# Routing and gathering the first 128 tokens while the second 128 are still being mapped, in an encoder trunk with experts

## The chip, the cores and the metric

The kernel runs on one core of one Trainium2 chip. Its engines are named as the profile names them: PE (matrix products, with PEld for the loading of its weights), DVE (the vector engine), ACT (the scalar engine), POOL (the general engine) and SP, which only issues transfers. The metric is the device time of one execution in microseconds (us). Three executions of the kernel before took 1431.76, 1432.56 and 1432.91 us; the median, 1432.56 us, is the time that the change is compared with. The profiled execution, from which all rows below come, took 1431.94 us, and its span in the trace is 1430.1 us.

## The reference, cut to what matters

Two layers act on 256 tokens of 1024 features. Layer 0 (retention and a dense SwiGLU) isn't touched apart from one small insertion. Layer 1 mixes the tokens by a two-dimensional Fourier transform with a linear map behind it, adds that to the residual, normalises, and sends each token to 2 of 8 experts:

```python
h = h + fourier_mixer(hn, fnet_w_out[j])          # the map: y.reshape(b, s, d) @ w_out
hn = rms_norm(h, ffn_norm[i])                     # y * rsqrt(mean(x^2) + eps) * g
h = h + moe_swiglu(hn, moe_router[j], moe_w_gate[j], moe_w_up[j], moe_w_down[j])

def moe_swiglu(h, w_router, w_gate, w_up, w_down):
    t = h.reshape(-1, d)
    logits = (t @ w_router).astype(jnp.float32)
    top_val, top_idx = lax.top_k(logits, TOP_K)
    top_w = jax.nn.softmax(top_val, axis=-1)
    gates = jnp.sum(jax.nn.one_hot(top_idx, N_EXPERTS) * top_w[..., None], axis=1)
    for e in range(N_EXPERTS):
        out = out + gates[:, e:e + 1] * swiglu(t, w_gate[e], w_up[e], w_down[e])
```

The norm's factor rsqrt(...) is one number for each token, so it changes neither which experts are largest nor their order; the kernel picks the experts from the rows multiplied by the gain g alone and puts the factor into the gates and the expert products later.

## The kernel before, in words

All arithmetic is float32 in two parts: a value is split into a high part (ACT copies it to the rounded type, `whi`, `nhi`, `xe`...) and a low part (DVE subtracts: `wlo`, `nlo`...), and a product is three matmuls, high by high, high by low, low by high (`mm3`, L247 to L250). The weights stream in pieces of 1 MB ("items" here). SP issues the transfer of an item as soon as one of its 11 to 15 buffers is free, ACT and DVE split an item in two halves each (L131, L132) into one of three pairs of buffers, and PE then takes 12 matmuls of 512 columns for it. There is no scheduler: each engine works its instructions in the order in which the code writes them, and waits where an operand is not there.

The tokens stand in two chunks of 128, c = 0 and 1, and the features in two halves of 512, hf = 0 and 1. The part around the change comes in this order.

- The map (`close`, L319). The last two items of `fnet_w_out` are applied group by group: (c, hf) = (0,0), (0,1), (1,0), (1,1), 12 matmuls each. After a group DVE adds its result to the residual `X` and multiplies it by the gain (`gained`, L261 to L268). One group later `r_sink` (L809) turns the gained half by four PE transposes, ACT copies them out (`xt`), ACT and DVE split the gained half into `nh`, `nl`, and ACT sums its squares. Two groups later the router's products run (`r_mm`, L768: four f32 matmuls of 8 columns, two passes each).
- The routing (`route`, L775): eight small DVE operations for a chunk find its two largest experts and write `mask`. PE counts, by a matmul with the triangular `upper`, the place `pos` of each token in its expert's list (L825 to L830); chunk 1 continues chunk 0's count through `ones`. `gates` (L786) works out the weights of the experts by some 20 tiny POOL operations.
- The gathering of the first two experts' tokens (`prep(0)`, L919): `choose` (L840) writes the 0/1 matrices `pm` on DVE, four tiles of 128x128; `gather` (L849) multiplies them with `nh` and `nl`, quarter by quarter (q = 0 to 3, each with both chunks, 8 matmuls of 256 columns), and splits each quarter into `xe`. All these tiles are in a pool `pe` that takes the memory of the pool before it, `pc`, and waits for all users of that pool.
- The experts, 56 steps of 512 hidden features (L1089 on). A step takes two items for the gate, two for the up product and two for the step before it down. The last part of `prep(0)`, `place` (L860: eight small passes that carry the gates to the gathered tokens), is run in step 0, between the first and the second item (L1104).

Of the kernel before, what the change touches and what calls it, by code (L numbers as in the profile page):

```python
# [12 lines left out]
OP = mybir.AluOpType  # L13
# [139 lines left out]
def body(nc, tc, a, out, upto=None):  # L153
    with ExitStack() as ctx:
# [76 lines left out]
        def route_consts(rw):  # L231
            nc.scalar.dma_start(rw, a["moe_router"][0].rearrange("(k p) e -> p k e", p=P))
            kw = dict(base=0, allow_small_or_imprecise_dtypes=True)
            ge.iota(iota8, pattern=[[1, NE]], channel_multiplier=0, **kw)
            ge.iota(slot, pattern=[[1, P]], channel_multiplier=0, **kw)
            ge.memset(ones, 1.0)
# [24 lines left out]
        def gained(c, hf, accs=None):  # L261


            x = X[:, c, HALF[hf]]
            if accs is not None:
                ve.tensor_add(x, x, accs[2 * c + hf])
            ve.tensor_mul(xgs[hf], x, gb[:, HALF[hf]])
            return xgs[hf]  # L268
# [50 lines left out]
        def close(its, accs, sink, early=None):  # L319
# [15 lines left out]
            return lambda: sink(*left)  # L335

# [272 lines left out]
        with tc.tile_pool(name="pb", bufs=1) as pb:  # L609
# [3 lines left out]
            tabd = pb.tile([P, 2, 512], F32, name="tabd", tag="hth", bufs=2)  # L613
            accs = [acc(i) for i in range(4)]
# [25 lines left out]
            for u in range(6):  # L640
# [22 lines left out]
                if u == 1:  # L663
                    split(td[0], td[1], tabd)
                hms[u] = []
# [35 lines left out]
        with tc.tile_pool(name="pc", bufs=1) as pc:  # L701
# [64 lines left out]
            sq, late = sq_tile(), []  # L766
# [42 lines left out]
            def r_sink(c, hf, xg):  # L809
                p = tr()  # L810
                for k in range(4):
                    te.transpose(p[:, cp(k)], xg[:, cp(k)], ident)
                se.copy(xt[c][:, 4 * hf:4 * hf + 4], p.rearrange("p (k t) -> p k t", k=4))
                for ch in late:
                    r_mm(*ch)
                late[:] = [(c, hf)]
                split(nh[:, c, HALF[hf]], nl[:, c, HALF[hf]], xg)
                square(sq, c, hf)

            left = close(its, accs, r_sink)  # L820
            po = mm("po")
            route(0)
            left()
            r_mm(1, 1)
            te.matmul(po[:, 0:8], upper, mask[:, 0], start=True, stop=True)  # L825
            route(1)
            ve.tensor_copy(pos[:, 0], po[:, :8])
            te.matmul(po[:, 8:16], ones, mask[:, 0], start=True, stop=False)
            te.matmul(po[:, 8:16], upper, mask[:, 1], start=False, stop=True)
            ve.tensor_copy(pos[:, 1], po[:, 8:16])  # L830
            gates()

# [5 lines left out]
        with tc.tile_pool(name="pe", bufs=1) as pe, tc.tile_pool(name="dr", bufs=1, space=bass.MemoryType.DRAM) as dr:  # L838
            pe = Aligned(pe)
            def choose(e0):  # L840

                pm = pe.tile([P, 2, 2 * P], F32R, name="pm")
                for c in range(2):
                    for j in range(2):
                        ve.tensor_scalar(pm[:, c, cp(j)], slot, pos[:, c, e0 + j:e0 + j + 1],
                                         mask[:, c, e0 + j:e0 + j + 1], op0=OP.is_equal, op1=OP.mult)
                return pm

            def gather(pm, xe, q, o=None):  # L849

                o = o or mm("ga")
                for i in range(2):
                    ds = cp(2 * q + i)
                    for c in range(2):
                        te.matmul(o[:, i * 256:(i + 1) * 256], nh[:, c, ds], pm[:, c], start=c == 0, stop=False)  # L855
                        te.matmul(o[:, i * 256:(i + 1) * 256], nl[:, c, ds], pm[:, c], start=False, stop=c == 1)  # L856
                ov = o.rearrange("p (i j s) -> p j i s", i=2, j=2)
                split(xe[:, :, 0, 2 * q:2 * q + 2], xe[:, :, 1, 2 * q:2 * q + 2], ov)

# [59 lines left out]
            def prep(e0):  # L919

                st = {}

                def first():
                    st["pm"] = choose(e0)
# [279 lines left out]
```

## Time and profile before

| | before |
|---|---|
| median of three runs | 1432.56 us |
| the profiled execution | 1431.94 us, span 1430.1 us |
| busy share of the span: PE, PEld, DVE, ACT, POOL | 98%, 82%, 81%, 68%, 5% |
| bytes read from memory | 431.54 MB |

The page's share of busy time is an average over stages that have different limits. PE is busy in nearly all of the span, so the reader looks for two things: the few places in which it isn't, and the places in which it works at a lower granted clock. A timeline row gives the start in us from the span's start, the duration in us (of all of the row's instructions, x how many), the engine, the line, the operation, output<-inputs and shape, and in brackets how long the engine had been idle and what ended it. Matmuls are pipelined: a duration is longer than the distance to the next start, and it is this distance that a matmul costs.

### The profile page before, as it was taken

The numbers are of one execution on the slowest core, as the hardware profiler recorded it, in microseconds if no ns is written. First come the engines' busy times: TensorE is split into PE (matmuls) and PEld (weight loads), VectorE is DVE, ScalarE is ACT, GpSimd is POOL, SyncE is SP. The second block draws the span as 40 slices with busy tenths as digits, with TensorE's granted clock in tenths as the row PEclk, the third lists the DMA queues.
The fourth block names the chain that finished last, engine by engine and source line by source line (L and its number), as shares of the span: only waits on it lengthen the run. The fifth ranks groups of instructions, "written<-read, shape, count | busy, mean of one in ns | idle before, by whom it ended". The sixth has DMA issues, their size and how long they took to land. (4 is left out here: it accounts for less than half of the span.)

```text
span 1430.1 us, 17313 instructions
## 1 busy us (share of the span) xinstructions
PE 1405.9 (98%) x6533; PEld 1166.7 (82%) x6533; DVE 1164.9 (81%) x1201; ACT 969.8 (68%) x1120; POOL 70.2 (5%) x109
## 2 busy tenths in 40 slices
PE   7999999999999999999999999999999999999997
PEld 6888878888888888888888888887878888888786
DVE  6866666545577999989999988998988898999996
ACT  5544446444455777777877777787777778778775
POOL 8400000000001000000000000000000000001000
PEclk9999999999999999999999999999999999999999
DMA  8646539755536989999999999999999999999990
GB/s 288 213 154 205 177 132 375 251 179 200 181 120 243 385 302 358 371 356 340 334 394 393 386 361 364 362 347 390 348 373 361 356 373 366 393 383 346 395 347 30
DMA packets 186700, 437.45 MB, mean 306 GB/s; under 512 B 8161, under 2 KB 10993, under 8 KB 186610
## 3 DMA queue, kind: packets, MB, share of 16 engines
q1 hardware_dynamic: 181424, 426.27, 81.7%
q10 hardware_dynamic: 4610, 7.92, 1.5%
q0 software_dynamic: 576, 2.10, 0.4%
q8 instruction: 52, 0.85, 0.2%
q14 instruction: 38, 0.31, 0.1%
HBM read 431.54 MB, written 4.72 MB: 305 GB/s over the span
## 5 line engine op out<-in xcount | busy, mean ns | idle before, releaser
L132 DVE TENSOR_TENSOR wlo<-raw,whi 128x1024 fp32r<-128x1024 f32 (+1 forms) x789 | 923.5, 1219 | 148.3 <-ACT whi L131 139.9
L131 ACT CAST whi<-raw 128x1024 fp32r<-128x1024 f32 (+1 forms) x789 | 786.1, 1047 | 200.7 <-PE acc L250 106.3
L248 PE MATMUL mm<-whi,xe 128*128 128x512 f32 x896 | 355.1, 396 | 0.3 <-PEq L1129 0.3
L250 PE MATMUL mm<-whi,xe 128*128 128x512 f32 x896 | 349.6, 390 | 0.0
L249 PE MATMUL mm<-wlo,xe 128*128 128x512 f32 x896 | 349.2, 390 | 0.0
L249 PE MATMUL acc<-wlo,hth 128*128 128x512 f32 x528 | 206.3, 391 | 2.3 <-DVE wlo L132 2.3
L248 PE MATMUL acc<-whi,hth 128*128 128x512 f32 x528 | 206.2, 391 | 0.0
L250 PE MATMUL acc<-whi,htl 128*128 128x512 f32 x528 | 206.1, 390 | 0.0
L250 PEld LDWEIGHTS mm<-whi,xe 128*128 128x128 f32 x896 | 168.2, 188 | 36.1
L248 PEld LDWEIGHTS mm<-whi,xe 128*128 128x128 f32 x896 | 168.4, 188 | 34.9 <-issue 2.2
L249 PEld LDWEIGHTS mm<-wlo,xe 128*128 128x128 f32 x896 | 168.5, 188 | 32.9
L248 PE MATMUL mm<-whi,nhi 128*128 128x512 f32 (+1 forms) x352 | 135.6, 385 | 0.0
L250 PE MATMUL mm<-whi,nlo 128*128 128x512 f32 (+1 forms) x352 | 133.9, 380 | 0.0
L249 PE MATMUL mm<-wlo,nhi 128*128 128x512 f32 (+1 forms) x352 | 133.7, 380 | 0.0
L249 PEld LDWEIGHTS acc<-wlo,hth 128*128 128x128 f32 x528 | 99.5, 188 | 23.3 <-DVE wlo L132 2.8
L250 PEld LDWEIGHTS acc<-whi,htl 128*128 128x128 f32 x528 | 99.5, 188 | 20.7
L248 PEld LDWEIGHTS acc<-whi,hth 128*128 128x128 f32 x528 | 99.6, 189 | 20.6
L253 ACT CAST hth<-tr 128x512 fp32r<-128x512 f32 (+1 forms) x67 | 38.9, 581 | 84.8 <-PE tr L294 84.8
L250 PEld LDWEIGHTS mm<-whi,nlo 128*128 128x128 f32 x352 | 66.2, 188 | 12.9
L249 PEld LDWEIGHTS mm<-wlo,nhi 128*128 128x128 f32 x352 | 66.3, 188 | 11.8
L248 PEld LDWEIGHTS mm<-whi,nhi 128*128 128x128 f32 x352 | 66.3, 188 | 11.9
L254 DVE TENSOR_TENSOR htl<-tr,hth 128x512 fp32r<-128x512 f32 (+1 forms) x67 | 45.7, 682 | 33.5 <-ACT hth L253 33.5
(291 smaller groups left out, 992.6 us busy)
## 6 DMA issues: line engine op xcount, KB each, us to landing
raw<-in_moe_w_gate SPq DMA_DIRECT2D x110, 1024.0 KB, 7.6
raw<-in_moe_w_down SPq DMA_DIRECT2D x108, 1024.0 KB, 7.6
raw<-in_moe_w_up SPq DMA_DIRECT2D x105, 1024.0 KB, 7.3
raw<-in_ret_w_in SPq DMA_DIRECT2D x23, 1024.0 KB, 5.2
raw<-in_dense_w_gate SPq DMA_DIRECT2D x11, 1024.0 KB, 5.3
raw<-in_dense_w_up SPq DMA_DIRECT2D x11, 1024.0 KB, 8.8
raw<-in_dense_w_down SPq DMA_DIRECT2D x11, 1024.0 KB, 6.6
raw<-in_ret_w_out SPq DMA_DIRECT2D x8, 1024.0 KB, 4.9
```

The source lines that it names most:

```text
L131: self.nc.scalar.copy(hi[sl], t[sl])
L132: self.nc.vector.tensor_sub(lo[sl], t[sl], hi[sl].bitcast(F32))
L248: te.matmul(o, lh, rh, start=first, stop=False)
L249: te.matmul(o, lh, rl, start=False, stop=False)
L250: te.matmul(o, ll, rh, start=False, stop=last)
L253: se.copy(hi, src)
L254: ve.tensor_sub(lo, src, hi.bitcast(F32))
```

## The change

The close of the map, the routing and the first gathering are written out as one sequence in which chunk 0 is ahead. `r_t` transposes `X` itself and not the gained half; to make up for that, the gain vector is loaded as 8 rows (`rg`), turned by one small PE transpose and multiplied into the router's weights during the dense layer. The gain product of chunk 1 goes to POOL (`gained(..., ge)`). `choose` and `gather` work on one chunk at a time: chunk 0's `mask`, `pos`, `pm` and its half of all four gathers run before chunk 1 is routed; three matmuls without a use (`warm`) stand ahead of chunk 1's half of the gathers. The `pm` of these gathers lies in the older pool `pt`, and POOL writes a second `pm` in pool `pe` for `place`, which runs behind the second item of step 0 and not behind the first. Pool `pe` is opened with `reuse_waits="tile"`: each of its tiles waits only for the users of its own bytes.

```diff
--- before.py
+++ after.py
@@ -230,6 +230,7 @@
 
         def route_consts(rw):
             nc.scalar.dma_start(rw, a["moe_router"][0].rearrange("(k p) e -> p k e", p=P))
+            nc.scalar.dma_start(rg[:8], a["ffn_norm"][1].rearrange("(k p) -> k p", p=P))
             kw = dict(base=0, allow_small_or_imprecise_dtypes=True)
             ge.iota(iota8, pattern=[[1, NE]], channel_multiplier=0, **kw)
             ge.iota(slot, pattern=[[1, P]], channel_multiplier=0, **kw)
@@ -258,13 +259,12 @@
             se.activation(hi, src, AF.Copy, scale=s)
             ve.scalar_tensor_tensor(lo, src, s, hi.bitcast(F32), op0=OP.mult, op1=OP.subtract)
 
-        def gained(c, hf, accs=None):
+        def gained(c, hf, accs, eng=None):
 
 
             x = X[:, c, HALF[hf]]
-            if accs is not None:
-                ve.tensor_add(x, x, accs[2 * c + hf])
-            ve.tensor_mul(xgs[hf], x, gb[:, HALF[hf]])
+            ve.tensor_add(x, x, accs[2 * c + hf])
+            (eng or ve).tensor_mul(xgs[hf], x, gb[:, HALF[hf]])
             return xgs[hf]
 
         scr = []
@@ -333,6 +333,19 @@
                         sink(*left)
                     left = (c, hf, xg)
             return lambda: sink(*left)
+
+        def choose(pm, e0, c, eng=None):
+
+            for j in range(2):
+                (eng or ve).tensor_scalar(pm[:, c, cp(j)], slot, pos[:, c, e0 + j:e0 + j + 1],
+                                          mask[:, c, e0 + j:e0 + j + 1], op0=OP.is_equal, op1=OP.mult)
+
+        def gather(o, pm, q, c):
+
+            for i in range(2):
+                ds = cp(2 * q + i)
+                te.matmul(o[:, i * 256:(i + 1) * 256], nh[:, c, ds], pm[:, c], start=not c and not i, stop=False)
+                te.matmul(o[:, i * 256:(i + 1) * 256], nl[:, c, ds], pm[:, c], start=False, stop=bool(c and i))
 
         def run(hooks, i):
             for f in hooks.get(i, ()):
@@ -611,6 +624,7 @@
             scratch(pb)
             tabr = pb.tile([P, 2, 2 * H1], F32, name="tabr")
             tabd = pb.tile([P, 2, 512], F32, name="tabd", tag="hth", bufs=2)
+            rg = pb.tile([P, P], F32, name="rg")
             accs = [acc(i) for i in range(4)]
             rst, sq = [], sq_tile()
 
@@ -662,6 +676,9 @@
                 o = dense_h(u)
                 if u == 1:
                     split(td[0], td[1], tabd)
+                    p = tr()
+                    te.transpose(p[:, :8], rg[:8], ident[:8, :8])
+                    ve.tensor_mul(rw, rw, p[:, :8, None].to_broadcast([P, 8, NE]))
                 hms[u] = []
                 for c in range(2):
                     t = pb.tile([P, 512], F32, name="hm", bufs=3)
@@ -763,7 +780,7 @@
 
             xt = [pc.tile([P, 8, P], F32, name="xt", tag="fh", bufs=2) for _ in range(2)]
             lgp = [mm("lg") for _ in range(2)]
-            sq, late = sq_tile(), []
+            sq = sq_tile()
 
             def r_mm(c, hf):
                 for k in range(4 * hf, 4 * hf + 4):
@@ -806,57 +823,87 @@
                 ge.tensor_add(gts[:, :, :NE], gts[:, :, :NE], g2)
                 ge.tensor_copy(gts[:, :, NE], rs)
 
-            def r_sink(c, hf, xg):
+            def maps(c, hf, i):
+                it, lh, ll = its[i]
+                out_mm(accs, it, lh, ll, c, False, i == 1, (hf,))
+
+            def r_t(c, hf):
+
                 p = tr()
                 for k in range(4):
-                    te.transpose(p[:, cp(k)], xg[:, cp(k)], ident)
+                    te.transpose(p[:, cp(k)], X[:, c, cp(4 * hf + k)], ident)
                 se.copy(xt[c][:, 4 * hf:4 * hf + 4], p.rearrange("p (k t) -> p k t", k=4))
-                for ch in late:
-                    r_mm(*ch)
-                late[:] = [(c, hf)]
-                split(nh[:, c, HALF[hf]], nl[:, c, HALF[hf]], xg)
-                square(sq, c, hf)
-
-            left = close(its, accs, r_sink)
-            po = mm("po")
+
+            def hi(c, hf):
+                se.copy(nh[:, c, HALF[hf]], xgs[hf])
+
+            def lo(c, hf):
+                ve.tensor_sub(nl[:, c, HALF[hf]], xgs[hf], nh[:, c, HALF[hf]].bitcast(F32))
+
+            def warm(n):
+
+                o = mm("warm")
+                for _ in range(n):
+                    te.matmul(o, nh[:, 0, :P], nh[:, 0, HALF[0]], start=True, stop=True)
+
+            for hf in range(2):
+                maps(0, hf, 0)
+                if hf:
+                    r_t(0, 0)
+                    hi(0, 0)
+                    lo(0, 0)
+                    square(sq, 0, 0)
+                maps(0, hf, 1)
+                gained(0, hf, accs)
+            maps(1, 0, 0)
+            r_t(0, 1)
+            hi(0, 1)
+            lo(0, 1)
+            square(sq, 0, 1)
+            r_mm(0, 0)
+            maps(1, 0, 1)
+            r_mm(0, 1)
+            gained(1, 0, accs, ge)
             route(0)
-            left()
+            maps(1, 1, 0)
+            r_t(1, 0)
+            hi(1, 0)
+            square(sq, 1, 0)
+            maps(1, 1, 1)
+            gained(1, 1, accs, ge)
+            po, pm = mm("po"), pt.tile([P, 2, 2 * P], F32R, name="pm0", tag="tdh")
+            te.matmul(po[:, 0:8], upper, mask[:, 0], start=True, stop=True)
+            r_mm(1, 0)
+            ve.tensor_copy(pos[:, 0], po[:, :8])
+            choose(pm, 0, 0)
+            r_t(1, 1)
+            square(sq, 1, 1)
+            hi(1, 1)
+            lo(1, 0)
+            go = [acc(q) for q in range(4)]
+            gather(go[0], pm, 0, 0)
             r_mm(1, 1)
-            te.matmul(po[:, 0:8], upper, mask[:, 0], start=True, stop=True)
+            for q in range(1, 4):
+                gather(go[q], pm, q, 0)
             route(1)
-            ve.tensor_copy(pos[:, 0], po[:, :8])
-            te.matmul(po[:, 8:16], ones, mask[:, 0], start=True, stop=False)
-            te.matmul(po[:, 8:16], upper, mask[:, 1], start=False, stop=True)
-            ve.tensor_copy(pos[:, 1], po[:, 8:16])
+            po = tr()
+            te.matmul(po[:, 0:8], ones, mask[:, 0], start=True, stop=False)
+            te.matmul(po[:, 0:8], upper, mask[:, 1], start=False, stop=True)
+            ve.tensor_copy(pos[:, 1], po[:, :8])
+            choose(pm, 0, 1)
             gates()
+            warm(3)
+            lo(1, 1)
+            for q in range(4):
+                gather(go[q], pm, q, 1)
 
         pt_.close()
         if upto == "C":
             return finish()
 
 
-        with tc.tile_pool(name="pe", bufs=1) as pe, tc.tile_pool(name="dr", bufs=1, space=bass.MemoryType.DRAM) as dr:
+        with tc.tile_pool(name="pe", bufs=1, reuse_waits="tile") as pe, tc.tile_pool(name="dr", bufs=1, space=bass.MemoryType.DRAM) as dr:
             pe = Aligned(pe)
-            def choose(e0):
-
-                pm = pe.tile([P, 2, 2 * P], F32R, name="pm")
-                for c in range(2):
-                    for j in range(2):
-                        ve.tensor_scalar(pm[:, c, cp(j)], slot, pos[:, c, e0 + j:e0 + j + 1],
-                                         mask[:, c, e0 + j:e0 + j + 1], op0=OP.is_equal, op1=OP.mult)
-                return pm
-
-            def gather(pm, xe, q, o=None):
-
-                o = o or mm("ga")
-                for i in range(2):
-                    ds = cp(2 * q + i)
-                    for c in range(2):
-                        te.matmul(o[:, i * 256:(i + 1) * 256], nh[:, c, ds], pm[:, c], start=c == 0, stop=False)
-                        te.matmul(o[:, i * 256:(i + 1) * 256], nl[:, c, ds], pm[:, c], start=False, stop=c == 1)
-                ov = o.rearrange("p (i j s) -> p j i s", i=2, j=2)
-                split(xe[:, :, 0, 2 * q:2 * q + 2], xe[:, :, 1, 2 * q:2 * q + 2], ov)
-
             def place(pm, last):
 
                 gl = pe.tile([P, 2, NE + 1], F32, name="gl", bufs=2)
@@ -920,16 +967,31 @@
 
                 st = {}
 
+                def maps(eng=None):
+                    st["pm"] = pe.tile([P, 2, 2 * P], F32R, name="pm")
+                    for c in range(2):
+                        choose(st["pm"], e0, c, eng)
+
                 def first():
-                    st["pm"] = choose(e0)
+                    if e0:
+                        maps()
                     st["xe"] = pe.tile([P, 2, 2, 8, P], F32R, name="xe", bufs=2)
                     for j in range(2):
                         XE[e0 + j] = st["xe"][:, j]
                 yield first
+
+                def part(q):
+                    o = mm("ga") if e0 else go[q]
+                    for c in range(2) if e0 else ():
+                        gather(o, st["pm"], q, c)
+                    ov, xe = o.rearrange("p (i j s) -> p j i s", i=2, j=2), st["xe"]
+                    split(xe[:, :, 0, 2 * q:2 * q + 2], xe[:, :, 1, 2 * q:2 * q + 2], ov)
                 for q in range(4):
-                    yield lambda q=q: gather(st["pm"], st["xe"], q, acc(q) if not e0 else None)
+                    yield lambda q=q: part(q)
 
                 def last():
+                    if not e0:
+                        maps(ge)
                     gl = place(st["pm"], e0 + 2 == NE)
                     for j in range(2):
                         GT[e0 + j] = gl[:, j, e0 + j:e0 + j + 1]
@@ -1101,7 +1163,7 @@
                 for s, o in enumerate(moe_h(e)):
                     if s == 0 and u:
                         hidden_t(u - 1)
-                    if s == 0 and not u:
+                    if s == 1 and not u:
                         work.pop(0)()
                 hm = pe.tile([P, 512], F32, name="hm")
                 se.activation(hm, o, AF.Silu, scale=RS[e])
```

PE's order from the last transposes on, before: `tr` holds transposes, `lg` the router's sums, `po` the counts, `acc_...` a gathered quarter.

```order
L812 MATMUL tr<-ident,gx 128x128 x4
L770 MATMUL lg<-rw,xt 128x8 x4
L812 MATMUL tr<-ident,gx 128x128 x4
L770 MATMUL lg<-rw,xt 128x8 x8
L825 MATMUL po<-mask,upper 128x8
L828 MATMUL po<-mask,ones 128x8
L829 MATMUL po<-mask,upper 128x8
L855 MATMUL acc_3569<-pm,nhi 128x256
```

PE's order after, from the last matmul of the map (`acc_3312`) to the second quarter of the first gather.

```order
L251 MATMUL acc_3312<-whi,yl 128x512
L875 MATMUL po<-mask,upper 128x8
L787 MATMUL lg<-rw,xt 128x8 x4
L834 MATMUL tr<-ident,X 128x128 x4
L347 MATMUL acc_3523<-pm_3505,nhi 128x256
L348 MATMUL acc_3523<-pm_3505,nlo 128x256
L347 MATMUL acc_3523<-pm_3505,nhi 128x256
L348 MATMUL acc_3523<-pm_3505,nlo 128x256
L787 MATMUL lg<-rw,xt 128x8 x4
L347 MATMUL acc_3524<-pm_3505,nhi 128x256
```

Chunk 0's count and gathers now stand among the last transposes and router products of chunk 1. PE's order after, from the last gather of chunk 0 to the first of chunk 1:

```order
L347 MATMUL acc_3526<-pm_3505,nhi 128x256
L348 MATMUL acc_3526<-pm_3505,nlo 128x256
L890 MATMUL tr<-mask,ones 128x8
L891 MATMUL tr<-mask,upper 128x8
L847 MATMUL warm<-nhi 128x512 x3
L347 MATMUL acc_3523<-pm_3505,nhi 128x256
L348 MATMUL acc_3523<-pm_3505,nlo 128x256
```

Only chunk 1's 16 gather matmuls are left behind the last count. POOL's order at the end of the gates, before (`k`, `ok` and `rv` are work for a much later stage):

```order
L806 TENSOR_TENSOR gts<-gts,g_3533 128x2x8
L807 COPY gts<-w 128x2
L882 TENSOR_SCALAR k_3927<-iota_94 128x8
L883 TENSOR_SCALAR ok<-pos 128x16
L884 MEMSET ok 128x2
```

and after:

```order
L823 TENSOR_TENSOR gts<-gts,g_3563 128x2x8
L824 COPY gts<-w 128x2
L340 TENSOR_SCALAR pm<-slot,pos,mask 128x128 x4
L929 TENSOR_SCALAR k_3942<-iota_94 128x8
L930 TENSOR_SCALAR ok<-pos 128x16
```

The four tiles of `pm` for `place` are now POOL's, behind the gates.

## Rows read from the trace of the kernel before

**Rows 1.** Windows: length, busy PE, PEld, DVE, ACT, POOL, granted clock, DMA share, GB/s.

```profile
443.00:450.00 7.00, 5.63 (x26) 5.57 (x27) 2.48 (x10) 1.17 (x2) 6.11 (x25) 0.51 0.59 209
```

**Rows 2.** Timeline of PE, from the map's second group to the expert items.

```profile
430.44 0.60 PE L812 MATMUL tr<-ident,gx 128*128 128x128 f32 x4
430.80 0.47 PE L248 MATMUL acc<-whi,yh 128*128 128x512 f32 x1
...
433.63 0.60 PE L812 MATMUL tr<-ident,gx 128*128 128x128 f32 x4
...
434.88 0.48 PE L248 MATMUL acc<-whi,yh 128*128 128x512 f32 x1
...
445.39 0.55 PE L855 MATMUL acc<-pm,nhi 128*128 128x256 f32 x1 [0.90 <-DVE pm L845]
...
451.18 0.28 PE L856 MATMUL acc<-pm,nlo 128*128 128x256 f32 x1
451.30 0.40 PE L248 MATMUL mm<-whi,xe 128*128 128x512 f32 x1
...
454.05 0.95 PE L872 MATMUL acc<-gts,pm 128*128 128x9 f32 x8
454.86 0.49 PE L248 MATMUL mm<-whi,xe 128*128 128x512 f32 x1
```

**Rows 3.** Timeline of ACT in the same stretch.

```profile
434.27 0.59 ACT L813 COPY xt<-tr 128x512 f32<-128x512 f32 x1 [1.46 <-PE tr L812]
...
440.14 0.59 ACT L813 COPY xt<-tr 128x512 f32<-128x512 f32 x1
...
451.98 5.79 ACT L131 CAST whi<-raw 128x1024 fp32r<-128x1024 f32 x6
```

**Rows 4.** Timeline of DVE in the same stretch.

```profile
428.57 0.68 DVE L266 TENSOR_TENSOR X<-X,acc 128x512 f32<-128x512 f32 x1
...
441.98 0.16 DVE L778 COPY lgt<-lg 128x8 f32<-128x8 f32 x1
...
443.12 0.23 DVE L784 SCALAR_TENSOR_TENSOR mask<-iota,if,o 128x8 f32<-128x8 f32 x1
...
444.53 0.17 DVE L830 COPY pos<-po 128x8 f32<-128x8 f32 x1 [1.11 <-PE po L829]
...
453.07 4.63 DVE L132 TENSOR_TENSOR wlo<-raw,whi 128x1024 fp32r<-128x1024 f32 x4 [0.26 <-ACT whi L131]
```

**Rows 5.** Timeline of POOL: one 128x128 operation, the gates' first and last.

```profile
408.01 0.56 POOL L752 TENSOR_SCALAR upper<-upper 128x128 f32<-128x128 f32 x1
...
441.95 0.20 POOL L792 TENSOR_TENSOR w<-sq 128x2 f32<-128x2 f32 x1 [33.34 <-ACT scr L281]
...
447.77 0.19 POOL L807 COPY gts<-w 128x2 f32<-128x2 f32 x1
```

**Rows 6.** Timeline of POOL at the kernel's start, beside DVE's splits.

```profile
17.62 0.20 POOL L384 TENSOR_TENSOR lu<-lu,lq 128x8 f32<-128x8 f32 x1
...
18.23 2.35 POOL L384 TENSOR_TENSOR lu<-lu,lq 128x8 f32<-128x8 f32 x1
...
32.21 4.73 POOL L419 TENSOR_SCALAR dm<-dpos,lg 128x512 f32<-128x512 f32 x1
...
38.65 1.29 POOL L422 TENSOR_TENSOR dm<-dm,dmb 128x512 f32<-128x512 f32 x1
```

**Rows 7.** Timeline of DVE at the kernel's start.

```profile
18.23 2.29 DVE L132 TENSOR_TENSOR wlo<-raw,whi 128x2048 fp32r<-128x2048 f32 x1 [0.78 <-ACT whi L131]
...
32.16 4.98 DVE L132 TENSOR_TENSOR wlo<-raw,whi 128x2048 fp32r<-128x2048 f32 x3 [0.48 <-ACT whi L131]
```

**Rows 8.** What SP waited for: total us, times, longest us.

```profile
SPq L105 <- DVE wlo L132: 1062.5, 358, 26.6
```

**Rows 9.** Timeline of PE where it waits longest in the expert stage.

```profile
1340.70 0.76 PE L249 MATMUL acc<-wlo,hth 128*128 128x512 f32 x1 [2.35 <-DVE wlo L132]
...
1344.22 0.39 PE L248 MATMUL acc<-whi,hth 128*128 128x512 f32 x1
```

## The prediction, made before the changed kernel had been run

> **What bounds the kernel now.** I read the windows around the change first, then the timelines of PE, ACT, DVE and POOL in that stretch, then two places elsewhere that show what the change will meet.
>
> PE bounds the kernel. In the expert stage an item of 12 matmuls takes 454.05 - 451.30 = 2.75 us, 0.229 us for each [rows 2], and SP's longest total wait is for buffers that DVE has yet to free, not for memory [rows 8]; transfers run ahead, so whatever moves the first expert item forward moves the end forward, as long as nothing behind it waits anew. Between the map and the experts lies the stretch that the change rewrites. There PE waits for DVE's `pos` and `pm` (0.90 us of idle ahead of 445.39 alone), and the granted clock is 0.51 from 443 to 450, that is about 1.2 of 2.4 GHz [rows 1, 2]. PE was idle or worked on matmuls of 8 columns before it fell. The 32 gathers take 451.30 - 445.39 = 5.91 us there; at the full clock, where one follows another after 0.12 us (451.18 to 451.30), they would take 3.84 [rows 2].
>
> **The change part by part: the new sequence.** I lay its instructions along the old starts.
>
> The map's second group has its first six matmuls done at 430.44 - 6 x 0.229 = 429.07, as before. Now the transposes of `X` (0,0) follow, and they need the addition that DVE starts at 428.57 and that takes 0.68 [rows 4]: PE waits 0.2 us, to 429.3. The other 30 matmuls of the map cost 6.87. Between them stand: transposes (0,0), 430.44 to 430.80 = 0.36, and 0.08 for the return to the map (12 matmuls from 430.80 end at 433.55, the next start is 433.63); transposes and router products of chunk 0, 434.88 - 433.63 = 1.25, and 0.08; router products alone, 1.25 - 0.36 = 0.89; transposes (1,0), 0.44 [rows 2]. The sum is 3.10, so the map ends at 429.3 + 6.87 + 3.10 = 439.3.
>
> Then two passes of `po` (0.2, a quarter of the eight passes above, an estimate) and the router products (1,0), 0.8: the last transposes start at 440.3. Their `X` is added by 439.3 + 0.2 + 0.68 = 440.2, just in time. ACT's copy starts 0.64 after the transposes do (433.63 to 434.27) and takes 0.59 [rows 2, 3]: 441.5. The last router products, 0.9 with their tail 0.15, let DVE start `route(1)` at 442.6. From its first operation to the end of `mask` it took 443.12 + 0.23 - 441.98 = 1.37 [rows 4]: 444.0. The count (two passes and their tail, 0.4, an estimate) brings `pos` at 444.4, and from `pos` to the first gather it was 445.39 - 444.53 = 0.86 [rows 2, 4]: 445.26. Sixteen gathers instead of 32 remain, 16 x 0.12 = 1.92, if the clock holds: the first expert item starts at 447.2 instead of 451.30, **-4.1 us**. Before that, chunk 0's gathers (4 at 441.0, 0.86 after its `pos` at 440.1, and 12 after 442.4) and the three `warm` matmuls (0.69, from 444.2) fill PE while it waits for ACT and DVE; they end by 443.9 and 445.0, ahead of what follows them. Were that cover gone, `warm` would cost its 0.69.
>
> The gain product of chunk 1 takes POOL 1.29 us (the same shape, L422) where DVE needs 0.68 [rows 4, 6]. That hides: `X` no longer goes through it to the transposes, and ACT's `nh` (1,1) needs it at about 442, the gathers at 446. The Trainium skill (GPSIMD Engine Reference, 4.1 Engine selection) speaks against it: it puts elementwise products on the vector engine and GpSimd at about half the speed. The rows agree, 1.29 against 0.68; by rule and by rows the sum stays the same, since nothing on the path waits for it.
>
> **The start of the experts.** ACT's first split starts 451.98 - 451.18 = 0.8 after the last gather, DVE's 453.07 - 451.98 = 1.09 later, and each half takes DVE 4.63 / 4 = 1.16 [rows 2, 3, 4]. After the change: 447.9, 449.0, and the two halves of the second item are ready at 450.2 and 451.4. PE reaches that item at 447.2 + 2.75 = 449.95 and now has no `place` in front of it to fill 454.86 - 454.05 = 0.81; its second matmul wants the first half at 450.2. Between 0.15 and 0.75 us (where POOL pushes DVE back by 0.3 in each half); I take **+0.4**.
>
> `place` then costs its 0.81 as before, but waits for four 128x128 operations on POOL. The gates take from 441.95 to 447.96, 6.0 us [rows 5]. They start when the squares of (1,1) are there: 441.95 - 440.14 = 1.8 after ACT's last copy began [rows 3, 5], less 0.5 for the `nh` copy that no longer stands between (an estimate, by the 0.59 of the copy of the same size): 440.9 + 1.3 = 442.2. So they end at 448.2; one low-part subtraction of DVE in between may hold a POOL step by 0.4: 448.6. Four operations at 0.56 [rows 5] would be done at 450.9, and PE comes at 453.1. But DVE works on weights without a pause from 449.0, and a POOL operation waits where such a subtraction runs: 8 columns took 0.20 us alone and 2.35 beside a `wlo` of 2.29 that started with them; a 512-column operation took 4.73 beside three of them [rows 6, 7]. The Trainium skill (GPSIMD Engine Reference, 1. Specifications) has the same: the SBUF interfaces are shared, with contention where DVE has two SBUF inputs, as `wlo` has. If each operation gets in at the next end of a subtraction, the first is done before 449.1 and the others at 450.8, 452.1 and 453.4: a stall of 0.3. If it misses every second end, as it seems to have done at 32.21, DVE's own stop limits the wait: after six halves, 449.0 + 7 = 456.0, it needs `place`'s result, POOL is free, and `place` is late by up to 3.5. Bounds 0 and 3.5; the small operations at the start mostly got in at the first end, so I take **+0.6**.
>
> **The dense layer.** One transpose of 8 rows more on PE, between nothing and the 0.36 of a set of four [rows 2]; I take **+0.25**, nearer to the upper end, as its weights are loaded for it alone. DVE's product of 64 columns stands ahead of two `hm`, where DVE has idle time. One tiny load on ACT's queue: nothing. The earlier loads into pool `pe` (SP's wait there shortens): nothing, since memory isn't waited for [rows 8].
>
> **The sum.** -4.1 + 0.25 + 0.4 + 0.6 = -2.85 us. Against the profiled execution's 1431.94: **1429.1 us**. The median of the runs shown lies 0.6 above that execution, their spread is 1.15, so I leave the number.
>
> **Rivals.**
>
> *Nothing waits.* The place is on time and the second item's halves are too: -4.1 + 0.25 + 0.15 = -3.7, 1428.2. For it: small POOL operations got through within a DVE step; against it: 32.21.
>
> *The clock falls all the same.* Between 439.3 and 445.3 PE has transposes, 8-column products and gaps of 0.1 to 0.3 us; before, the fall came in such work and waiting [rows 1, 2]. Then the 16 gathers cost 0.21 each instead of 0.12 (5.91 for 32, most of them slow), +1.5, and the first items run slow until it rises, at most +1.5 more, half of what was low after: with one of them in the middle, -2.85 + 2.2, 1431.3. Against it: 28 matmuls of 256 columns and three of 512 stand in that stretch where there were none.
>
> *POOL's second `pm` decides, and the kernel gets slower.* At `place` PE stalls for 3.5 us because DVE's weight subtractions lock POOL out. A stall of 2.35 at 1340.70 was followed by eight matmuls in 1344.22 - 1340.70 = 3.52 us, 3.52 - 8 x 0.229 = 1.7 us more than at the usual distance [rows 9]. Then -4.1 + 0.25 + 0.4 + 3.5 + 1.7 = +1.75, 1433.7. For it: 4.73 at 32.21. It decides from a stall of 2 us on; the point where all gain is gone is 3.4 with the clock as it is.
>
> *It doesn't do what it says.* If DVE's 128-column `choose` waits for POOL's product at 440.2, chunk 0's gathers come 1 us later, and with them chunk 1's router products, which stand behind them on PE: -1.85, 1430.1.
>
> **How the numbers follow.** The forecast has 0.43, nothing waits 0.2, the clock 0.13, the slow place 0.14, the late first gather 0.1. The measurement can tell about 0.2%, 2.9 us, from no change. Faster by more than that: all of "nothing waits" but a little, and two thirds of the forecast, which lies at that bound: 0.48. Within it: the rest of the forecast, the clock, the late gather and half of the slow place, less 0.03 for what I haven't seen: 0.42. Slower by more: the other half of the slow place, with over 1 us on top, and those 0.03: 0.10. The range reaches from 1427.2 (nothing waits, and 1 us better than laid out) to 1433.6 (most of the slow place).
>
> **What would show it.** In the profile after: the first expert matmul at about 447.2 and the granted clock 1.00 from 439 to it; the gathers' rows at 0.12 us apart; POOL's four `pm` and the end of PE's wait at `place`; the wait of the second item for `wlo`. The prediction is wrong if the first expert matmul is earlier than 446 or later than 449, if PE waits at `place` for over 2 us, or if the expert stage gains or loses time behind step 0.

## The result: 0.73% slower, and the profile after

The changed kernel takes 1441.51 us, the median of five runs (1440.11 to 1444.97), against 1432.48 us of the kernel before beside it. The ratio over all runs is 1.0073, with a 95% interval from 1.0061 to 1.0084; the two medians alone give 1.0063. The prediction was 1429.1, at most 1433.6.

The profiled execution of after took 1444.21 us, with a span of 1442.4, 12.3 more than before's 1430.1. To see where, I set the start of the same PE instruction in both traces against each other, at the transposes of each hidden tile:

| point in the program | later than before, us | grown by |
|---|---|---|
| dense layer, step 0 | 6.07 | 6.07 |
| dense layer, step 1, up to the map | 6.49 | 0.42 |
| expert stage, step 1 | 11.56 | 5.07 |
| behind the branch, about 1011 | 13.18 | 1.62 |
| last steps | 12.31 | -0.87 |

The fourth row is no work of the change: PE waits 1.96 us at the branch before and 1.98 after, and in this execution of after the granted clock fell to 0.50 behind that wait. Nor is the fifth: the fall of the clock behind the wait of 2.35 us at 1340.70 before [rows 9] doesn't come in after, where the same wait took 2.43. The profiled run is also the second slowest of the five, so the medians, 9.0 apart, are the fairer size.

**The dense layer.** ACT's timeline in after; ACTq rows are the issues of loads, the second number is how long one took:

```profile
225.08 0.39 ACTq L667 DMA_DIRECT2D tabr<-in_dft_s  x1
225.50 0.49 ACTq L668 DMA_DIRECT2D tabd<-in_dft_d  x1
226.08 0.42 ACTq L219 DMA_DIRECT2D gx<-in_mix_norm  x1
226.54 0.44 ACTq L232 DMA_DIRECT2D rw<-in_moe_router  x1
227.03 4.88 ACTq L233 DMA_DIRECT2D rg<-in_ffn_norm  x1
232.01 1.27 ACT L674 ACTIVATE gs<-mm,rs 128x512 f32<-128x512 f32 x2 [6.22 <-issue]
```

The new load of 4 KB holds ACT's queue for 4.88 us, and ACT's `gs` behind it starts at 232.01. The list of what PE waited for (total, times, longest) shows who pays, and the second of the new waits as well:

```profile
PE mm L249 <- ACT gs L674: 4.2, 1, 4.2
...
PE acc L919 <- POOL pm L340: 1.8, 1, 1.8
```

The wait of 4.2 us is not all of the 6.07. Behind it the granted clock fell (the third number from the end of this row of windows), and nine matmuls from 233.31 to 236.96 stood 0.41 us apart instead of 0.227, 1.6 us more:

```profile
234.00:236.00 2.00, 2.00 (x6) 1.57 (x5) 1.76 (x2) 1.16 (x2) 0.00 (x0) 0.50 1.02 392
```

**From the router to the experts.** PE's timeline in after; taking 6.49 off each start sets it against [rows 2]:

```profile
446.86 0.63 PE L834 MATMUL tr<-ident,X 128*128 128x128 f32 x4
448.51 0.58 PE L347 MATMUL acc<-pm,nhi 128*128 128x256 f32 x1 [1.01 <-DVE pm L340]
...
449.53 1.71 PE L787 MATMUL lg<-rw,xt 128*128 128x8 f32 x8
451.09 0.56 PE L347 MATMUL acc<-pm,nhi 128*128 128x256 f32 x1
...
457.59 0.40 PE L249 MATMUL mm<-whi,xe 128*128 128x512 f32 x1
...
463.38 0.73 PE L919 MATMUL acc<-gts,pm 128*128 128x9 f32 x6
465.93 0.60 PE L919 MATMUL acc<-gts,pm 128*128 128x9 f32 x2 [1.82 <-POOL pm L340]
466.38 0.77 PE L249 MATMUL mm<-whi,xe 128*128 128x512 f32 x1
...
472.07 0.55 PE L250 MATMUL mm<-wlo,xe 128*128 128x512 f32 x1
```

The first expert matmul is at 457.59 - 6.49 = 451.10, where it was at 451.30 before. `place` starts at 463.38 and the next item at 466.38, 3.00 us later instead of 0.81. The 13 matmuls from 466.38 to 472.07 stand 5.69 / 13 = 0.44 apart instead of 0.229. The windows of after say why (the third number from the end of a row is the granted clock):

```profile
446.00:448.00 2.00, 1.50 (x14) 1.26 (x13) 1.94 (x3) 0.84 (x3) 1.15 (x1) 1.00 0.00 0
448.00:450.00 2.00, 1.49 (x7) 1.49 (x8) 1.05 (x3) 1.24 (x4) 1.24 (x5) 0.62 0.00 0
450.00:452.00 2.00, 2.00 (x10) 2.00 (x11) 0.62 (x5) 0.00 (x0) 0.45 (x3) 0.50 0.00 0
...
456.00:458.00 2.00, 2.00 (x17) 1.96 (x16) 1.07 (x3) 1.60 (x4) 0.94 (x5) 1.00 0.03 8
...
466.00:468.00 2.00, 2.00 (x6) 1.71 (x7) 0.74 (x2) 1.23 (x2) 1.78 (x8) 0.50 1.03 410
```

In this stretch PE drops from 2.4 to 1.2 GHz twice: about 448.5, after the transposes and 1.01 us of idle, and again at the end of its wait at `place`. Before, it fell once here [rows 1].

Both waits come from DVE and POOL side by side. DVE in after, beside [rows 4]:

```profile
446.83 1.63 DVE L340 TENSOR_SCALAR pm<-slot,pos,mask 128x128 fp32r<-128x128 f32 x2
...
454.89 0.60 DVE L340 TENSOR_SCALAR pm<-slot,pos,mask 128x128 fp32r<-128x128 f32 x2
...
459.43 7.17 DVE L132 TENSOR_TENSOR wlo<-raw,whi 128x1024 fp32r<-128x1024 f32 x6
```

POOL in after, its second `pm` operation by operation, beside [rows 5, 6]:

```profile
446.85 1.26 POOL L267 TENSOR_TENSOR gx<-X,gx 128x512 f32<-128x512 f32 x1 [2.79 <-ACT scr L281]
...
457.87 0.81 POOL L340 TENSOR_SCALAR pm<-slot,pos,mask 128x128 fp32r<-128x128 f32 x1 [0.97 <-PE acc L348]
458.67 0.80 POOL L340 TENSOR_SCALAR pm<-slot,pos,mask 128x128 fp32r<-128x128 f32 x1
459.45 2.93 POOL L340 TENSOR_SCALAR pm<-slot,pos,mask 128x128 fp32r<-128x128 f32 x1
462.36 3.51 POOL L340 TENSOR_SCALAR pm<-slot,pos,mask 128x128 fp32r<-128x128 f32 x1
```

While POOL's gain product ran, DVE's two `choose` operations took 1.63 us; without it, 0.60. While DVE's weight subtractions ran, POOL's `pm` took 2.93 and 3.51 each, and the last ended at 465.87, during the sixth subtraction (its end is at 466.60). The engine that was ahead kept its time: 1.26 us for the product, against 1.29 [rows 6], and 7.17 / 6 = 1.20 for a subtraction, against 1.16 [rows 4]. The Trainium skill (Trainium Architecture — The Big Picture, What this means for kernel authors) calls the port pair of these two engines an exclusive lock and not a split of bandwidth; by these rows the trace agrees, in both directions.

### The profile page after: what moved, and what is told of

Its sections match the earlier page's. It is cut to its first block, busy times and chain, and to the rows that moved or that the text cites. A ratio compares the mean times of both kernels' runs of the same rounds, so it can differ in the third digit from the quotient of the medians.

```text
span 1442.4 us, 17325 instructions
## 1 busy us (share of the span) xinstructions
PE 1414.4 (98%) x6537; PEld 1171.3 (81%) x6537; DVE 1165.2 (81%) x1200; ACT 969.4 (67%) x1120; POOL 80.8 (6%) x115
```

## The experiments

Medians here are set against the kernel before on the same chip, 1431.6 to 1432.1.

### The new load

*before_rg* is the kernel before with this load alone:

```
     nc.scalar.dma_start(rw, a["moe_router"][0].rearrange("(k p) e -> p k e", p=P))
+    nc.scalar.dma_start(rg[:8], a["ffn_norm"][1].rearrange("(k p) -> k p", p=P))
```

> The kernel before with one addition: the load of rg as the fifth on ACT's queue; what it brings is not used. Theory 1: its issue takes about 4.9 us, PE waits some 4.2 us longer for the first gs, and the time rises from 1432.5 by about 6 to 1438.5. Rival (the stall needs something else of the change, the order of the pools for one): no change, 1432.5 within 1.5.

1438.43 us, ratio 1.0048 (1.0035 to 1.0061). The issue took 4.88 us, PE waited 4.16 us for `gs`, and the first step came 5.90 us later. The load alone costs 6 us.

*rg_late* is the changed kernel with that load behind `gs`:

```
     gs.append(t)
+if not u:
+    nc.scalar.dma_start(rg[:8], ...)
```

> The changed kernel with one edit: the load of the weights rg is issued on ACT's queue after the dense layer's first two gs operations instead of as the fifth of five loads ahead of them. Theory 1 (it is the place in the queue that costs: the fifth load's issue holds ACT for 4.88 us, and PE waits 4.2 us for gs): issued late it takes about 0.5 us as the others do, PE's wait at the first gs goes, and the time falls by 6.1 us, 1441.5 to 1435.4. Rival (the load is slow to issue wherever it stands): it takes 4.9 us behind gs, holds back ACT's weight splits there, and the time stays within 2 us of 1441.5.

1435.13 us, 1.0025 (1.0017 to 1.0034): 6.1 expected, 6.4 measured (6.0 where each kernel is taken against the kernel before beside it). But theory 1 had the issue at 0.5 us, and it was as slow as in after and ended when it had ended there (about 232). ACT in rg_late:

```profile
227.25 4.79 ACTq L676 DMA_DIRECT2D rg<-in_ffn_norm  x1
227.72 0.68 ACT L673 ACTIVATE gs<-mm,rs 128x512 f32<-128x512 f32 x1
232.08 3.91 ACT L131 CAST whi<-raw 128x1024 fp32r<-128x1024 f32 x4 [3.68 <-issue]
```

The weight splits behind it had that much slack: PE waited for nothing. So the gain comes from the place behind `gs`, not from a faster issue; what holds the issue is asked next.

*rg_first*: the same load first of the five.

```
+nc.scalar.dma_start(rg[:8], ...)
 nc.scalar.dma_start(tabr, ...)
```

> The changed kernel with the load of rg first of the five loads on ACT's queue; the router's weights rw become the fifth. Theory 1a (the queue takes four loads, whatever they are, and the fifth issue waits until the first has landed): now rw takes about 4.9 us to issue, PE waits as before, 1441.5 within 1.5. Rival 1b (what holds rg's issue is the load ahead of it, rw with its 1024 pieces of 32 bytes): all five are issued in 0.4 to 0.7 us each, and the time falls by about 6 to 1435.4.

1434.28 us, 1.0017 (1.0008 to 1.0026), near rival 1b's 1435.4. Theory 1a falls; five loads go out without a stop. ACT in rg_first:

```profile
225.13 0.30 ACTq L666 DMA_DIRECT2D rg<-in_ffn_norm  x1
...
226.94 0.44 ACTq L232 DMA_DIRECT2D rw<-in_moe_router  x1
227.49 1.26 ACT L674 ACTIVATE gs<-mm,rs 128x512 f32<-128x512 f32 x2 [1.64 <-POOL ones L236]
```

*rw_second*: the changed kernel with the router's weights second.

```
 nc.scalar.dma_start(tabr, ...)
+nc.scalar.dma_start(rw, ...)
 nc.scalar.dma_start(tabd, ...)
```

> The changed kernel with the load of the router's weights rw second of the five on ACT's queue, and rg still last. Theory 1b (the issue that stands behind rw's 1024 pieces is held until they are taken): now tabd, which stands behind it, takes 4 to 5 us to issue, and gx and rg about 0.45. Rival (it is the fifth load behind some amount of bytes that is held): rg takes 4.9 us again, tabd 0.5. In both PE waits about as long for the first gs, and the time is that of the changed kernel, 1441.5 within 3.

1437.23 us in its one run. The stall moved to whatever stands behind `rw`, and is shared by two loads. ACT in rw_second:

```profile
225.44 0.49 ACTq L667 DMA_DIRECT2D rw<-in_moe_router  x1
...
225.97 2.63 ACTq L668 DMA_DIRECT2D tabd<-in_dft_d  x1
228.69 1.27 ACTq L219 DMA_DIRECT2D gx<-in_mix_norm  x1
230.00 0.37 ACTq L232 DMA_DIRECT2D rg<-in_ffn_norm  x1
```

So the place as fifth isn't the cause. But the stall is smaller than I expected, 3.0 us over the usual 0.49 and 0.42 of these two instead of about 4, PE's wait was 2.67 us and not as long as in after, and the time is outside the 1441.5 within 3 that theory and rival both gave.

*rw_whole*: the fourth load brings the same 32 KB in 128 pieces instead of 1024; the old load of `rw` follows behind `gs`.

```
-nc.scalar.dma_start(rw, a["moe_router"][0].rearrange("(k p) e -> p k e", p=P))
+nc.scalar.dma_start(rwd, a["moe_router"][0].rearrange("(p k) e -> p k e", k=8))
```

> The changed kernel with the fourth of the five loads replaced by one of the same 32 KB in 128 pieces of 256 bytes, into a tile that nothing reads; the router's weights themselves are loaded by the old load of 1024 pieces, as a sixth behind the two gs operations. rg stays fifth. Theory 1c (it is the number of pieces ahead of an issue that holds it): rg now takes about 0.4 us, gs starts at 227.5, and the time is about that of rg_late, 1435. The sixth load itself isn't held either, as in the kernel before. Rival (the bytes, or the place as fifth, hold it): rg takes 4 to 5 us again and the time is 1441.5 within 2.

1434.92 us, 1.0021 (1.0012 to 1.0031), as theory 1c has it. ACT in rw_whole:

```profile
226.41 0.44 ACTq L232 DMA_DIRECT2D rwd<-in_moe_router  x1
226.89 0.35 ACTq L233 DMA_DIRECT2D rg<-in_ffn_norm  x1
227.34 1.26 ACT L675 ACTIVATE gs<-mm,rs 128x512 f32<-128x512 f32 x2 [1.69 <-POOL ones L237]
228.40 0.40 ACTq L678 DMA_DIRECT2D rw<-in_moe_router  x1
```

With the same bytes in the same place, 1024 pieces ahead of an issue hold it 4.9 us, and 128 pieces don't. The load with the many pieces is itself issued in 0.40. Theory 1b's "until they are taken" isn't shown, though. The list of loads in after has, for `rw`, its size and the time from issue to landing:

```profile
rw<-in_moe_router ACTq DMA_DIRECT2D x1, 32.0 KB, 16.5
```

So `rw` landed at about 243, some 11 us after the held issue had ended (227.03 + 4.88). What ends the hold stays open, and so does whether it is the number of the pieces or their size that counts.

### POOL's second pm and place

*rg_first* has a second answer. In its profile the clock stayed at 1.00 through the router, and the first expert matmul came 2.7 us earlier than in rg_late's profile (448.83 against 451.56). PE's wait at `place` took back part of it. Three timelines of rg_first, in this order PE, DVE and POOL:

```profile
448.83 0.40 PE L248 MATMUL mm<-whi,xe 128*128 128x512 f32 x1
...
458.23 0.39 PE L919 MATMUL acc<-gts,pm 128*128 128x9 f32 x2 [2.88 <-POOL pm L339]
```

```profile
450.68 6.99 DVE L132 TENSOR_TENSOR wlo<-raw,whi 128x1024 fp32r<-128x1024 f32 x6
```

```profile
449.29 8.88 POOL L339 TENSOR_SCALAR pm<-slot,pos,mask 128x128 fp32r<-128x128 f32 x4
```

POOL began 1.4 us ahead of DVE and still ended 0.5 us behind DVE's six subtractions; in after it ended 0.7 us before their end. An earlier start of POOL didn't bring `place` forward: it had to wait for about the end of DVE's six in both.

*late_place* is rg_late without that second `pm`: `place` for the first two experts stands right behind the last gather and reads chunk 0's and 1's first one.

```
     for q in range(4):
         gather(go[q], pm, q, 1)
+    for j in range(2):
+        for c in range(2):
+            te.matmul(pl[:, 16 * j:16 * j + NE + 1], pm[:, c, cp(j)].bitcast(F32), gts[:, c], ...)
...
-        if not e0:
-            maps(ge)
```

> rg_late with a second edit: the gains and scales of the first two experts' tokens are taken with chunk 0's and 1's first pm right after the last gather, on PE, and POOL's second pm and the place behind the first expert item are gone. Theory 3 (POOL's pm, which waits for the last gather and is locked out by DVE's weight subtractions, costs PE 1.8 us at place and then a fall of the clock worth 0.2 us in each of 12 matmuls): the expert stage has no stall and no fall there, -1.8 - 2.6 = -4.4 against rg_late: 1431.0. Rival (the clock falls at the start of the experts in any case, or DVE's weight stream is what PE waits for): PE waits for wlo or hm instead, and the time stays within 1.5 us of rg_late's, 1435.4.

1429.96 us, 0.9990 (0.9982 to 0.9999). Theory 3 expected -4.4 against rg_late and got -5.2 at the medians; the two profiles have 3.9 of it at step 1. In the first expert step PE waits for nothing and the clock is 1.00, though it had fallen ahead of it as in after. Two windows of late_place:

```profile
444.00:446.00 2.00, 2.00 (x10) 2.00 (x11) 0.65 (x5) 0.00 (x0) 0.44 (x3) 0.50 0.00 0
...
452.00:454.00 2.00, 2.00 (x12) 1.74 (x12) 2.00 (x5) 2.00 (x3) 0.82 (x5) 1.00 0.29 26
```

### The clock, the gain product and the rest

*dve2* is late_place with the last gain product on DVE, behind `choose`:

```
-gained(1, 1, accs, ge)
+gained(1, 1, accs, add=True)
...
 choose(pm, 0, 0)
+ve.tensor_mul(xgs[1], X[:, 1, HALF[1]], gb[:, HALF[1]])
```

> late_place with one more edit: the gain product of the last quarter (1,1) is taken from POOL and stands on DVE behind chunk 0's two choose operations. Theory 2 (POOL's product holds DVE's choose, which took 1.62 us there instead of 0.60, and so the first gather): choose takes 0.60, the first gather starts at 441.5 instead of 442.5, and the first expert matmul comes 1.0 us earlier if the clock goes the same way, 3 us or more if it holds: 1429.0 from 1430.0, or 1426.5. Rival (chunk 1's last router products wait for ACT's copy, so an earlier gather brings nothing): the time stays within 0.5 us of 1430.0.

1430.68 us (1429.10 to 1431.79), 0.9990 (0.9981 to 0.9999): no gain over late_place. Its timelines, first DVE, then PE:

```profile
440.97 0.60 DVE L341 TENSOR_SCALAR pm<-slot,pos,mask 128x128 fp32r<-128x128 f32 x2
```

```profile
441.63 0.39 PE L348 MATMUL acc<-pm,nhi 128*128 128x256 f32 x1
...
449.49 1.06 PE L906 MATMUL tr<-gts,pm 128*128 128x9 f32 x8 [1.16 <-POOL gts L827]
450.40 0.48 PE L248 MATMUL mm<-whi,xe 128*128 128x512 f32 x1
```

The mechanism is as theory 2 has it: `choose` takes 0.60, the first gather starts at 441.63 instead of 442.48. The time isn't: `place` now stands ahead of the experts, and PE waits 1.16 us for the gates that POOL ends last.

*fill* is late_place with `warm(4)` ahead of the first gather; *nowarm* is late_place without `warm(3)`.

> late_place with four more matmuls of 512 columns ahead of the first gather, where PE is idle for 1.01 us (0.92 us of work, their result is not used). Theory C1 (that idle microsecond is what lets the clock fall): the granted clock is 1.00 from 436 to the experts, the gathers stand 0.12 apart throughout, and the first expert matmul comes about 3 us earlier, as in rg_first's profile where the clock held: 1427.2. Rival C2 (the fall comes with the 8-column router products, whatever stands ahead of them, and in some runs only): the clock falls as before at 443 to 449, the time stays within 1 us of 1430.0.

> late_place without the three matmuls called warm ahead of chunk 1's gathers; nothing that is returned depends on them. Theory W1 (they bring the clock up): without them chunk 1's gathers run 0.21 apart instead of 0.12, +1.5, and the first expert matmuls slowly: 1431.5 to 1433. Rival W2 (they only fill a wait for pm, and the clock rises with the gathers as well): the time stays within 0.7 us of 1430.0.

*fill*: 1429.43 us (1429.10 to 1430.82), 0.9982 (0.9973 to 0.9991). Its profile has the granted clock at 1.00 in every window from 436 to 470, the gathers 0.12 apart, and the first expert matmul at 450.23 instead of late_place's 452.35. The median came down by 0.5 and not by the 2.8 that C1 expected. Six of late_place's eleven runs are at 1429.2 to 1430.0, as low as fill's; rg_first's profile had the same idle microsecond and kept its clock. So the idle doesn't decide alone, and by the times C1 isn't shown. The profiles lean its way: where there is no idle ahead of the first gather (dve2, fill, lg, lg_fill) the clock held through the router in all four, and where there is 1.01 us of it, it fell in five (after, rg_late, late_place, nowarm, rw_whole) and held in two (rg_first, rw_second). That is one execution of each kernel.

*nowarm*: 1432.68 us (1429.97 to 1436.69), 1.0004 (0.9994 to 1.0015). The time is where W1 put it, but not for its reason: in the profile, an execution of 1432.49, the clock fell at the router, yet chunk 1's gathers ran 0.12 apart, and step 1 came 0.95 us earlier than in the kernel before. The time went at the branch, where the clock fell to 0.50 in this execution and 1.6 us were lost, as in after. The mean granted clock of each execution is on record too: 0.997 to 0.998 in the four at 1430.0, 0.991 to 0.993 in the four above 1435. So the spread goes with the clock; where it fell in those four, and what `warm` has to do with it, stays open.

*lg* is dve2 with the first `pm` in a pool of its own, so that `place` can stand behind the first expert item; *lg_fill* is the same with fill's edit in place of dve2's.

```
-pm = pt.tile([P, 2, 2 * P], F32R, name="pm0", tag="tdh")
+pm = p0.tile([P, 2, 2 * P], F32R, name="pm0", tag="tsl")
...
+gl = place(st["pm"] if e0 else pm, e0 + 2 == NE)
```

> dve2 with chunk 0's and 1's first pm kept in a place of its own, so that place stands behind the first expert item again, as in the changed kernel, but reads that first pm, and POOL makes no second one. Theory G (in dve2's profile PE waits 1.16 us ahead of the experts for the gates that POOL ends at 449.2, because place stands there): the first expert matmul starts at 448.2 instead of 450.4, place costs its 0.8 behind the item, so step 1 and the end come 1.4 us earlier: 1429.3 from 1430.7 (in the profile a span near 1427.7). Rival (place's result is then read behind six weight subtractions on DVE, ACT's first hm and the splits queued behind it wait, and PE waits for weights in step 0): no gain, 1430.7 or up to 1 us more.

> lg with the gain product (1,1) back on POOL and four matmuls of 512 columns ahead of the first gather, as in fill. Theory C1 with G: the clock holds in nearly every run, the first expert matmul starts at 448.8 instead of fill's 450.2, -1.4 and +0.8 for place being counted in both: 1428.5 from 1429.4, spread under 2 us. Rival: as for lg, PE waits for weights in step 0, 1429.4 or more.

*lg*: 1430.51 us, 0.9989 (0.9980 to 0.9998); *lg_fill*: 1430.52 us, 0.9993 (0.9984 to 1.0002): the rival, both times. The timelines of lg, first PE, then ACT:

```profile
447.89 0.39 PE L248 MATMUL mm<-whi,xe 128*128 128x512 f32 x1
...
463.90 0.66 PE L295 MATMUL tr<-ident,hm 128*128 128x128 f32 x4 [0.99 <-DVE hm L1177]
```

```profile
456.89 0.69 ACT L1173 ACTIVATE hm<-mm,gl 128x512 f32<-128x512 f32 x1 [2.43 <-DVE gl L927]
```

The experts start 2.3 us earlier than in fill (447.89 against 450.23), but `gl` waits behind six subtractions on DVE, ACT's `hm` and the splits behind it wait for `gl`, and PE waits for the second `hm` (0.94 us in lg_fill). At step 1 lg is 1.99 us ahead of the kernel before, and fill 1.94.

*before_reuse*: the kernel before with `reuse_waits="tile"` alone.

> The kernel before with one part of the change alone: the expert pool's tiles wait by tile instead of for the whole pool ahead of them. Theory: weights are loaded earlier at the start of the experts, but PE does not wait for memory there, so no change: 1432.1 within 1. Rival: the earlier loads or splits bring the second item's halves forward, -0.5 to -1.

1432.76 us, 1.0002 (0.9993 to 1.0011): no change. In the changed order of instructions this part wasn't tried by itself.

The lowest median is fill's: the change with the load of `rg` behind `gs`, `place` read from the first `pm`, and four matmuls whose result is not used. It is 0.18% faster than the kernel before (0.09 to 0.27) and 12 us faster than the change. Its interval overlaps those of late_place, dve2 and lg, so that it is better than they isn't shown.

## Why the prediction was wrong, point by point

**"One tiny load on ACT's queue: nothing."** This step failed first, and by most: 6.07 us. The sum put the load at nothing without a row for it, and asked neither what it stands behind (a load of 1024 pieces, which held its issue 4.88 us) nor what stands behind it (`gs`, for which PE waited 4.2 us; matmuls at half the clock took most of the rest).

**The transpose and product of `rg`:** +0.25 predicted, 0.42 measured.

**The new sequence, -4.1 "if the clock holds".** In after it gave -0.2. Where the clock held (rg_first's profile) it gave 448.83 - 0.45 - 451.30 = -2.9; the 0.45 is how late the map was. So the clock cost about 2.7 of the 3.9 missing, by these two executions. The rival that named it had a price of 2.2, but on chunk 1's gathers and the first items; those ran at full clock in after, and it was paid in chunk 0's gathers and in the router products (1.71 us for eight, against 0.95 in rg_first), on which the routing of chunk 1 waits. The other 1.2 lies mostly in the rival "late first gather", which I gave 0.1: the profile shows `choose` held to 1.63 us by POOL's gain product, dve2 shows 0.60 without it, and there the last gather comes 0.8 earlier than in rg_first, each taken from its own map. I wrote that the product hides because nothing waits for its result. What waited was DVE, while POOL worked. My rows [rows 6, 7] show POOL held beside DVE; I didn't ask whether it works in the other direction too.

**The second item, +0.4:** it waited 460.71 - 460.33 - 0.23 = 0.15 us in after.

**`place`, +0.6, bounds 0 and 3.5.** It took 2.19 us longer than its 0.81, inside the bounds, but the 13 matmuls behind it ran at half the clock and cost 5.69 - 13 x 0.229 = 2.7 more. The steps that failed are the choice between the ends and the clock, which the +0.6 left out. I took POOL operations of 8 columns, which got in between two subtractions, as nearest; the row of the 512-column operation [rows 6], which took 4.73 beside three, was the nearer one. The rival "POOL's second `pm` decides" had the whole mechanism, with the fall of the clock, and I gave it 0.14. I let it decide from a stall of 2 us on; here the clock fell with one of 1.82.

**The earlier loads:** nothing predicted, nothing measured (before_reuse, alone).

So three of the rivals came true together, which none of my sums had, and a step priced at nothing was larger than any of them. At medians: 6.4 us by the load (rg_late), 5.2 by POOL's `pm` and `place` (late_place). Without both, the change gains 2.1 us. That this is near the 2.85 of my sum is partly luck: `place` stands elsewhere there, and in late_place's profile, where the clock fell at the router, step 1 comes 0.2 us later than before; it is fill's profile, where the clock held, that has step 1 earlier by 1.94.

Open: why the clock falls behind a wait in some executions and not behind the same wait in others, the 1.6 us behind the branch among them.

## What to carry to other kernels

Read for each added transfer what stands ahead of it on its queue, and count the pieces of that one, not its bytes alone; a transfer of many small pieces goes last, with no engine work on the critical path behind the next issue. Work given to GpSimd beside a stream of VectorE operations that read SBUF twice was done only about when that stream ended, and one such operation held a short VectorE one 1.0 us: price it in both directions. And price a stall of PE of some 2 us together with the slow matmuls that can follow it; behind `place` they cost 2.7 us in after's profile and 1.6 in rg_late's, beside a stall of 1.82 in both.

## What the runs showed of the hardware

- An issue on ACT's queue took 4.88 us behind a load of 1024 pieces of 32 bytes, and 0.35 behind the same 32 KB in 128 pieces of 256. The Trainium skill (Perfetto Trace Analysis, DMA Instruction — HWDGE (DVE, Sync)) says that the profiled window of an issue ends once its descriptors have been generated, and that more may be generated than fit in the descriptor buffer. A wait for room there would look like these rows; no run here shows the buffer itself.
- A 128x128 operation of POOL took 0.80 us beside DVE's `xe` subtractions, which read one operand from PSUM, and 2.93 and 3.51 beside weight subtractions, which read both from SBUF. The Trainium skill (GPSIMD Engine Reference, 1. Specifications) names two SBUF inputs, and a 2-port mode, as the cases of contention; for the first, the trace agrees. DVE's `choose`, which has one large operand, was held as well, 1.63 us instead of 0.60; in which mode it ran no run shows.
